# Output gates summed along rows and spread through a DRAM row, in a two-layer hybrid decoder trunk

## The chip, the core and the metric

The kernel runs on one NeuronCore of one Trainium2 chip: one TensorE, one VectorE, one ScalarE, one GpSimd, the SyncE (SP) whose queue issues most transfers, and 16 DMA engines. The metric is the device time of one execution in microseconds; the median of several runs is compared.

## The reference

Two layers of a decoder trunk on one sequence of 256 positions with a model width of 1024, all in float32. Each layer has three sub-layers: a feed-forward network (SwiGLU, 2816 hidden), a token mixing sub-layer (chunked spatial gating, sparse attention, a short convolution), and a second feed-forward network. Every sub-layer is wrapped in the same way; shift, scale and gate come from the conditioning vector c:

```python
c_act = jax.nn.silu(c)
for l in range(DEPTH):
    mod = (c_act @ mod_w[l] + mod_b[l]).reshape(Bsz, 9, D_MODEL)
    h = pre_norm_modulate(x, norm_g[l, 0], mod[:, 0], mod[:, 1])
    x = post_norm_residual(x, swiglu(h, ffn_w13[l, 0], ffn_w2[l, 0]), norm_g[l, 1], mod[:, 2], MACARON_W)
    h = pre_norm_modulate(x, norm_g[l, 2], mod[:, 3], mod[:, 4])
    y = token_mixing(h, ...)
    x = post_norm_residual(x, y, norm_g[l, 3], mod[:, 5], 1.0)
    ...

def post_norm_residual(x, y, g, gate, res_w):
    return x + res_w * gate[:, None, :] * rmsnorm(y, g)
```

The change concerns the six gates mod[:, 2], mod[:, 5] and mod[:, 8] of the two layers: each is a vector of 1024 values, the product of silu(c) with a 1024 x 1024 block of mod_w, plus a bias. It is multiplied by res_w (0.5, or 1 in token mixing) and by the norm weight norm_g before it scales y.

## The kernel before

**Weights.** The weights lie in DRAM in the order of their use, in 284 blocks of 128 partitions x 2048 float32 (1 MB). `load` (L148) issues one block on SP's queue into one of three `raw` buffers. For a matmul, `units` (L155) splits each half of the block into a rounded part `hi` (ScalarE, L162) and a remainder `lo` (VectorE, L163), eight buffers of each. `mm3` (L167) multiplies with three matmuls, hi x hi, hi x lo and lo x hi (L168 to L170), which adds up to nearly full precision.

**Sub-layers.** In `ffn` (L343) the 11 column chunks of the first weight are multiplied, passed through SwiGLU (`gate_t`, L349), transposed (`chunk_end`, L357) and multiplied by the second weight (`down`, result `yf`). In `mixing` (L485) the query and first key-value projections (`uA`, `uq`) come first, then the second key-value projection (`uB`, result `kvb`, blocks cB0 and cB1), then the compression weights `cw1` (matmuls `ph`, L754), then the attention heads. The other branches are a long generator, `bulk` (L509), whose matmuls fill in between the attention's by `fill` (L632); its first result is `cg`. At a sub-layer's end, `finish` (L313) calls `post` (L255) for each half of the positions: the norm's power of -0.5 is taken on GpSimd (`rstd`, L246), `u` is y times the gate tile (L261, L263), and x is updated (L265). `norm` (L267) scales the new x into `xn` (L274), which TensorE transposes (`xT`, L283) for the next sub-layer.

**Conditioning.** The products with silu(c) are no matmuls. At the start silu(c) is made in two forms: `cact`, 8 columns of 128 (L132 to L136), and `crow`, one row spread over all partitions by a matmul (L137 to L145). `mod_cols` (L178) makes shift and scale of a sub-layer as columns: the weight block is transposed on the host, so that one VectorE instruction multiplies it with `crow` and sums along the row (`accum_out`, L187). `mod_gate` (L198) makes a gate. A tile `acc` is cleared by GpSimd (L200) and its first partition loaded with the bias (L201). Four blocks h0 to h3 bring eight weight tiles, each multiplied by a column of `cact` and added to `acc` (L206). Then `acc` is split into `ah` (ScalarE, L212) and `al` (VectorE, L213), and matmuls with a matrix of ones (L218, L219) sum the 128 partitions and spread the sum over them. The result is multiplied into the tile `o`, named gate, which holds the norm weights, loaded on SP's queue (L210, a 4 KB row read by 128 partitions).

**Order.** Both functions are generators: every `yield` ends a step, and `mod_step` (L226) runs the next steps of a queue of jobs at places written out by hand. A gate has five steps: one for each of h0 to h2, one for h3 with the work up to `al`, one for the matmuls. In `ffn` the steps come between chunks. In `mixing` the places are counted by `MIX_STEP`: `MIX_STEP[0]` after the first two projections (L644), `[1]` and `[2]` inside the `kvb` projection after its 4th and 10th product (L724, L729), `[3]` after it (L732), `[4]` to `[11]` inside `bulk`. The order of the program gives priorities; a planner then sorts each engine's instructions by them and by the times at which it expects the operands, and places the waits. Each engine and each queue executes its list in that order.

Of the kernel before, what the change touches and what calls it, by code (L numbers as in the profile page):

```python
# [17 lines left out]
L = 2  # L18
S = 256
D = 1024  # L20
FF = 2816
P = 128
# [20 lines left out]
AFTER = (0, 0, 2, 3, 4, 5, 6, 6)  # L43
N0 = 4
S2 = 9
MIX_STEP = (2, 1, 1, 1, 0, 0, 0, 0, 1, 2, 2, 2)

N_PAIRS = L * (2 * 33 + 40 + 36)

# [22 lines left out]


@with_exitstack
def trunk(ctx: ExitStack, tc: tile.TileContext, order, x_in, c_in, wst, smalls, gmws, ng_rows, modb, lnrows, rope_c, mask_c, out):
    nc = tc.nc
    E = ctx.enter_context
    cp = E(tc.tile_pool(name="cp", bufs=1))
    rawp = E(tc.tile_pool(name="rawp", bufs=RAW_BUFS))
    wp = E(tc.tile_pool(name="wp", bufs=UNIT_BUFS))  # L80
    sp = E(tc.tile_pool(name="sp", bufs=1))
    ps_y = E(tc.tile_pool(name="ps_y", bufs=4, space=PSUM))
    ps_m = E(tc.tile_pool(name="ps_m", bufs=2, space=PSUM))
    ps_t = E(tc.tile_pool(name="ps_t", bufs=2, space=PSUM))
    V, A, G, T = nc.vector, nc.scalar, nc.gpsimd, nc.tensor

    def s4(name, shape=(P, NT, 512), dt=F32):
        return sp.tile(list(shape), dt, name=name, tag="s4", bufs=S4)
# [16 lines left out]
    def t_tile(name):  # L105
        return ps_t.tile([P, 512], F32, name=name, tag="t")


    sizes = [("cT", 8), ("ngT", L * 3 * 8), ("mbT", L * 6 * 8), ("conv", L * 12), ("pe", L * 32), ("bs", L * 4), ("cw2", L * 256)]
    tot = sum(n for _, n in sizes)  # L110
    sml = cp.tile([P, tot], F32, name="sml")
    early = 8 + L * 3 * 8 + L * 6 * 8
    crow1 = s4("crow1", (1, D))
    nc.sync.dma_start(crow1, c_in)
    nc.sync.dma_start(sml[:, :early], smalls[:, :early])
    view, at = {}, 0
# [8 lines left out]
    ones_r = cp.tile([P, P], F32R, name="ones_r")  # L125
# [3 lines left out]

    kcB = cp.tile([P, 2, 30], F32, name="kcB")  # L130
    G.memset(kcB, 0.0)
    cact = cp.tile([P, 8], F32, name="cact")  # L132
    cth = cp.tile([P, 8], F32, name="cth")
    A.activation(cth, view["cT"], AF.Tanh, scale=0.5)
    V.scalar_tensor_tensor(out=cact, in0=cth, scalar=1.0, in1=view["cT"], op0=ALU.add, op1=ALU.mult)
    V.tensor_scalar(cact, cact, 0.5, None, op0=ALU.mult)  # L136
    crow2 = s4("crow2", (1, D))  # L137
    A.activation(crow2, crow1, AF.Tanh, scale=0.5)
    V.scalar_tensor_tensor(out=crow2, in0=crow2, scalar=1.0, in1=crow1, op0=ALU.add, op1=ALU.mult)
# [1 line left out]
    crow = cp.tile([P, D], F32, name="crow")  # L141
    for h in range(2):
        pt = t_tile("crow")
# [4 lines left out]
    def load(desc, cols=2048):  # L148
        i = len(order)
        order.append(desc)  # L150
        raw = rawp.tile([P, 2048], F32, name="raw", tag="raw")
        nc.sync.dma_start(raw[:, :cols], wst[i, :, :cols])
        return raw
# [18 lines left out]
    def rows(ap2, n):  # L172
        return bass.AP(tensor=ap2.tensor, offset=ap2.offset, ap=[[0, P], [1, n]])
# [22 lines left out]
        yield  # L196

    def mod_gate(l, i):  # L198
        acc = s4("acc", (P, D))
        G.memset(acc, 0.0)  # L200
        G.dma_start(acc[0:1, :], modb[l, 3 * i + 2])  # L201
        for h in range(4):
            raw = load(("mod", l, 3 * i + 2, h))
            for u in range(2):
                k = 2 * h + u
                V.scalar_tensor_tensor(out=acc, in0=raw[:, u * D : (u + 1) * D], scalar=cact[:, k : k + 1], in1=acc, op0=ALU.mult, op1=ALU.add)  # L206
            if h < 3:
                yield
        o = cp.tile([P, D], F32, name="gate", tag="gate", bufs=1)
        nc.sync.dma_start(o, rows(ng_rows[l, i], D))  # L210
        ah, al = s4("ah", (P, D), F32R), s4("al", (P, D), F32R)
        A.activation(ah, acc, AF.Copy)  # L212
        V.tensor_tensor(al, acc, ah.bitcast(F32), ALU.subtract)  # L213
        yield
        for h in range(2):
            pt = t_tile("modg")
            hs = slice(h * 512, (h + 1) * 512)
            T.matmul(pt, lhsT=ones_r, rhs=ah[:, hs], start=True, stop=False)  # L218
            T.matmul(pt, lhsT=ones_r, rhs=al[:, hs], start=False, stop=True)  # L219
            V.scalar_tensor_tensor(out=o[:, hs], in0=pt, scalar=1.0 if i == 1 else 0.5, in1=o[:, hs], op0=ALU.mult, op1=ALU.mult)  # L220
        mods[(l, i, "g")] = o
        yield

# [2 lines left out]
    def mod_step(n=1):  # L226
        for _ in range(n):
            while jobs:
                try:
                    next(jobs[0])  # L230
                    break
                except StopIteration:
                    jobs.popleft()
# [251 lines left out]
    def mixing(l, hT, pend, nxt):  # L485
        def in_units(lo_c, n):
            return units(("in", l, ((lo_c, n),), 0)) + units(("in", l, ((lo_c, n),), 1))
# [21 lines left out]
        def bulk():  # L509
            def run(us, name, evac, hooks, **kw):  # L510
                for k, _ in enumerate(chunk_steps(evac, us, name, **kw)):
                    if k in hooks:
                        hooks[k]()
                    yield
# [3 lines left out]
            yield from run(in_units(C0 + 1024, 512), "xt", lambda t, p: V.tensor_tensor(h2[:, t], h2[:, t], p, ALU.mult), {})  # L518
            mod_step(MIX_STEP[4])
            h2T, cv = s4("h2T", (P, 4, S)), s4("cv", (P, 4, S))  # L520
# [20 lines left out]

            mod_step(MIX_STEP[5])
            ws = s2("ws", (P, 4, P))
# [198 lines left out]
        for kind in range(2):  # L742
# [4 lines left out]
            pe = view["pe"][:, (l * 2 + kind) * 16 : (l * 2 + kind + 1) * 16]  # L747
            pe = pe.unsqueeze(2).unsqueeze(3).to_broadcast([P, 16, 2, 15])
# [16 lines left out]
            A.activation(x, pg[:, :30], AF.Copy)  # L765
            h30.append(x)
        fill(F1)
        w2 = [view["cw2"][:, (l * 2 + kind) * P : (l * 2 + kind + 1) * P] for kind in range(2)]
        po = t_tile("po")
        T.matmul(po[:, :30], lhsT=w2[0], rhs=h30[0], start=True, stop=True)  # L770
        for i in range(2):
# [2 lines left out]
        h120 = s2("h120", (P, 2, 4, 15))  # L774
        A.activation(h120, h30[1].rearrange("p (g n) -> p g n", g=2).unsqueeze(2).to_broadcast([P, 2, 4, 15]), AF.Copy)
        po = t_tile("po")
        T.matmul(po[0:120, :64], lhsT=h120.rearrange("p g h n -> p (g h n)"), rhs=w2[1][:, :64], start=True, stop=True)
        A.activation(vc[:, 0], po[0:120, :64], AF.Copy, scale=0.5)
        V.scalar_tensor_tensor(out=vc[:, 1], in0=po[0:120, :64], scalar=0.5, in1=vc[:, 0].bitcast(F32), op0=ALU.mult, op1=ALU.subtract)
        fill(F1)  # L780
# [103 lines left out]
        for i in range(len(heads) + 4):  # L884
            if i < len(heads):
                t, h = heads[i]
# [78 lines left out]
def pack(inp, order):  # L965
    import numpy as np

    st = np.zeros((N_PAIRS, P, 2048), np.float32)

    def put(i, blocks):  # L970
        at = 0
        for b in blocks:
            st[i, :, at : at + b.shape[1]] = b
            at += b.shape[1]

    def kt(w, k):
        return w[k * P : (k + 1) * P]

    for i, d in enumerate(order):
        kind, l = d[0], d[1]  # L980
        if kind == "w13":
            w, j = inp["ffn_w13"][l, d[2]], d[3]
            cols = [(256 * j, 256), (FF + 256 * j, 256)]
            put(i, [kt(w, k)[:, c : c + n] for k in range(4 * d[4], 4 * d[4] + 4) for c, n in cols])
        elif kind == "w2":
            put(i, [kt(inp["ffn_w2"][l, d[2]], 2 * d[3] + k) for k in range(2)])
        elif kind == "in":
            w = inp["w_in"][l]
            put(i, [kt(w, k)[:, c : c + n] for k in range(4 * d[3], 4 * d[3] + 4) for c, n in d[2]])
        elif kind == "gate":  # L990
            w, c = inp["w_gate"][l], D * d[2] + 512 * d[3]
            put(i, [kt(w, k)[:, c : c + 512] for k in range(4 * d[4], 4 * d[4] + 4)])
        elif kind == "br":
            put(i, [kt(inp["w_branch"][l, d[2]], k)[:, 512 * d[3] : 512 * d[3] + 512] for k in range(4)])
        elif kind == "out":
            put(i, [kt(inp["w_out"][l], 2 * d[2] + k) for k in range(2)])
        elif kind == "cw1":
            put(i, [kt(inp["cmp_w1"][l, d[2]], k) for k in range(16)])
        elif kind == "mod":
            put(i, [kt(inp["mod_w"][l], 2 * d[3] + k)[:, D * d[2] : D * d[2] + D] for k in range(2)])  # L1000
        else:
            w = inp["mod_w"][l]
            put(i, [w[:, D * (3 * d[2] + j) + P * d[3] : D * (3 * d[2] + j) + P * d[3] + P].T for j in range(2)])
    return st
# [39 lines left out]
```

## Time and profile before

| | us |
|---|---|
| median of 3 runs (1299.84 to 1302.82) | 1302.6 |
| the profiled execution's own time | 1301.73 |
| span of that execution in the profile | 1300.0 |
| TensorE busy in the span | 1266.7 |
| VectorE busy | 1026.8 |
| ScalarE busy | 681.4 |
| GpSimd busy | 31.2 |
| mean granted TensorE clock, share of full speed | 0.996 |

The profile is of one execution. Starts are counted from the beginning of the span. Matmuls are pipelined: the duration of one is longer than the distance to the next. An instruction's row names the tile that it writes, an arrow, and the tiles that it reads.

### The profile page before, as it was taken

The numbers are of one execution on the slowest core, as the hardware profiler recorded it, in microseconds if no ns is written. First come the engines' busy times: TensorE is split into PE (matmuls) and PEld (weight loads), VectorE is DVE, ScalarE is ACT, GpSimd is POOL, SyncE is SP. The second block draws the span as 40 slices with busy tenths as digits, with TensorE's granted clock in tenths as the row PEclk, the third lists the DMA queues.
The fourth block names the chain that finished last, engine by engine and source line by source line (L and its number), as shares of the span: only waits on it lengthen the run. The fifth ranks groups of instructions, "written<-read, shape, count | busy, mean of one in ns | idle before, by whom it ended". The sixth has DMA issues, their size and how long they took to land.

```text
span 1300.0 us, 15997 instructions
## 1 busy us (share of the span) xinstructions
PE 1266.7 (97%) x5940; PEld 1041.0 (80%) x5940; DVE 1026.8 (79%) x1628; ACT 681.4 (52%) x1135; POOL 31.2 (2%) x53
## 2 busy tenths in 40 slices
PE   6999999999999999999999999999999999999997
PEld 4788888888778878888878888887877887888886
DVE  7977997789999698867589768586989896885553
ACT  5453446566475464544465445456674564554442
POOL 1000001000000010000010000010000000100000
PEclk9999999999999999999999999999999999999999
DMA  8966884765467448767559767366545673684540
GB/s 334 365 237 236 338 321 171 259 235 202 146 246 260 190 178 338 282 249 267 190 205 331 289 240 279 141 245 247 219 163 194 246 276 126 254 311 168 188 165 33
DMA packets 43905, 304.31 MB, mean 234 GB/s; under 512 B 5169, under 2 KB 5425, under 8 KB 8498
## 3 DMA queue, kind: packets, MB, share of 16 engines
q1 hardware_dynamic: 43634, 303.26, 62.6%
q8 instruction: 47, 0.77, 0.2%
q14 instruction: 32, 0.26, 0.1%
q0 software_dynamic: 192, 0.02, 0.0%
HBM read 302.21 MB, written 1.05 MB: 233 GB/s over the span
## 4 chain that ended last, share of the span: by engine, by line
PE 81%; DVE 9%; issue 4%; ACT 3%; DMA 2%; POOL 1%; SPq 0%; POOLq 0%; DVEq 0%; ACTq 0%
PE gu L170 11%; PE gu L168 11%; PE gu L169 11%; PE yf L170 5%; PE yf L168 5%; PE yf L169 5%; DVE lo L163 3%; PE gt L169 3%; PE gt L168 3%; PE gt L170 3%; DMA raw<-w_dram 2%; PE hT L361 1%; PE ph L754 1%; PE br L168 1%; DVE raw L187 1%
## 5 line engine op out<-in xcount | busy, mean ns | idle before, releaser
L163 DVE TENSOR_TENSOR lo<-raw,hi 128x1024 fp32r<-128x1024 f32 (+1 forms) x416 | 496.8, 1210 | 120.1 <-ACT hi L162 115.8
L162 ACT ACTIVATE hi<-raw 128x1024 fp32r<-128x1024 f32 (+1 forms) x416 | 424.7, 1048 | 235.2 <-DMA raw<-w_dram 111.6
L168 PE MATMUL gu<-hi,hT 128*128 128x512 f32 x704 | 278.9, 397 | 3.9 <-ACT hT L410 3.9
L169 PE MATMUL gu<-lo,hT 128*128 128x512 f32 x704 | 275.2, 391 | 1.7 <-DVE lo L163 1.7
L170 PE MATMUL gu<-hi,hT 128*128 128x512 f32 x704 | 275.6, 392 | 0.0
L168 PEld LDWEIGHTS gu<-hi,hT 128*128 128x128 f32 x704 | 132.7, 189 | 31.7 <-ACT hT L410 4.6
L170 PEld LDWEIGHTS gu<-hi,hT 128*128 128x128 f32 x704 | 132.5, 188 | 29.6 <-DVE hT L411 0.7
L169 PEld LDWEIGHTS gu<-lo,hT 128*128 128x128 f32 x704 | 133.0, 189 | 29.0 <-DVE lo L163 2.5
L168 PE MATMUL yf<-hi,hid 128*128 128x512 f32 x352 | 137.6, 391 | 0.0
L169 PE MATMUL yf<-lo,hid 128*128 128x512 f32 x352 | 137.2, 390 | 0.0
L170 PE MATMUL yf<-hi,hid 128*128 128x512 f32 x352 | 137.0, 389 | 0.0
L187 DVE SCALAR_TENSOR_TENSOR raw<-raw,crow 128x1024 f32<-128x1024 f32 x96 | 114.9, 1217 | 3.5 <-DMA raw<-w_dram 2.9
L353 ACT ACTIVATE ht<-gu 128x256 f32<-128x256 f32 x88 | 33.4, 383 | 158.8 <-PE gu L170 158.8
L354 DVE SCALAR_TENSOR_TENSOR ht<-ht,gu 128x256 f32<-128x256 f32 x88 | 36.4, 416 | 59.8 <-ACT ht L353 59.8
L170 PEld LDWEIGHTS yf<-hi,hid 128*128 128x128 f32 x352 | 66.1, 188 | 13.7
L169 PEld LDWEIGHTS yf<-lo,hid 128*128 128x128 f32 x352 | 66.1, 188 | 13.6
L168 PEld LDWEIGHTS yf<-hi,hid 128*128 128x128 f32 x352 | 66.1, 188 | 13.4
L168 PE MATMUL gt<-hi,hT 128*128 128x512 f32 x192 | 76.1, 396 | 0.4 <-DVE v L498 0.4
L169 PE MATMUL gt<-lo,hT 128*128 128x512 f32 x192 | 75.1, 391 | 0.3 <-DVE lo L163 0.2
L170 PE MATMUL gt<-hi,hT 128*128 128x512 f32 x192 | 75.1, 391 | 0.0
L206 DVE SCALAR_TENSOR_TENSOR acc<-raw,cact,acc 128x1024 f32<-128x1024 f32 x48 | 61.4, 1279 | 1.0 <-DMA raw<-w_dram 0.6
L821 ACT ACTIVATE pr<-sc,mx 128x128 f32<-128x128 f32 (+1 forms) x64 | 26.2, 415 | 38.4 <-DVE mx L818 38.2
(295 smaller groups left out, 1810.1 us busy)
## 6 DMA issues: line engine op xcount, KB each, us to landing
raw<-w_dram SPq DMA_DIRECT2D x276, 1024.0 KB, 4.8
raw<-w_dram SPq DMA_DIRECT2D x4, 816.0 KB, 4.3
gate<-ng_dram SPq DMA_DIRECT2D x6, 512.0 KB, 5.4
raw<-w_dram SPq DMA_DIRECT2D x4, 768.0 KB, 4.5
x<-x_dram SPq DMA_DIRECT2D x2, 512.0 KB, 4.2
ln<-ln_dram SPq DMA_DIRECT2D x2, 512.0 KB, 5.6
ws<-gmws_dram SPq DMA_DIRECT2D x2, 256.0 KB, 5.0
out_dram<-x SPq DMA_DIRECT2D x1, 512.0 KB, 2.8
```

The costliest lines, as they stand in the source:

```text
L162: A.activation(hi[:, :width], src, AF.Copy)
L163: V.tensor_tensor(lo[:, :width], src, hi[:, :width].bitcast(F32), ALU.subtract)
L168: T.matmul(o, lhsT=xh, rhs=wh, start=start, stop=False)
L169: T.matmul(o, lhsT=xh, rhs=wl, start=False, stop=False)
L170: T.matmul(o, lhsT=xl, rhs=wh, start=False, stop=stop)
L187: V.scalar_tensor_tensor(out=raw[:, j * D : (j + 1) * D], in0=raw[:, j * D : (j + 1) * D], scalar=1.0, in1=crow, op0=ALU.mult, op1=ALU.mul ...
L206: V.scalar_tensor_tensor(out=acc, in0=raw[:, u * D : (u + 1) * D], scalar=cact[:, k : k + 1], in1=acc, op0=ALU.mult, op1=ALU.add)
L353: A.activation(h, pm[:, :256], AF.Tanh, scale=0.5)
L354: V.scalar_tensor_tensor(out=h, in0=h, scalar=1.0, in1=pm[:, :256], op0=ALU.add, op1=ALU.mult)
L361: T.transpose(out=pt[:, k * S + t * P : k * S + (t + 1) * P], in_=st[j]["h"][:, t, k * P : (k + 1) * P], identity=ident)
L754: T.matmul(ph[:30, :P], lhsT=blk[:, k].rearrange("p g n -> p (g n)"), rhs=w1[:, k * P : (k + 1) * P], start=k == 0, stop=k == 15)
L821: A.activation(pr[:, br], sc[:, br], AF.Exp, scale=0.125, bias=mx[:, br : br + 1], accum_out=nsum[:, br : br + 1])
```

## The change

A gate is now made like a shift or a scale. The host transposes the weight block in such a way that partition p of the block holds the weights of the outputs 8p to 8p+7. One VectorE instruction for each of the eight tiles multiplies with `crow` and sums along the row into one column of `col`, a tile of 16 columns of which 8 are used (two copies make 128 bytes). The bias and the norm weights come as columns `mbG` and `ngG` with the small inputs, so two instructions on 8 columns finish the gate. GpSimd's queue then writes the 128 x 8 values into a 4 KB row in DRAM, in the order of the outputs, and in the next step reads this row into all 128 partitions of `o`. `acc`, `ah`, `al`, the matmuls, `cact` and the loads of bias and norm weights are gone. The compression weights `cw2` are stored in 192 columns instead of 256 per layer, and the early small inputs grow from 152 to 240 columns. `MIX_STEP` changes from 2, 1, 1, 1 to 0, 3, 1, 1 at its first four places; the total stays.

```diff
-MIX_STEP = (2, 1, 1, 1, 0, 0, 0, 0, 1, 2, 2, 2)
+MIX_STEP = (0, 3, 1, 1, 0, 0, 0, 0, 1, 2, 2, 2)
...
+    dp = E(tc.tile_pool(name="dp", bufs=1, space=bass.MemoryType.DRAM))
...
-    sizes = [("cT", 8), ("ngT", L * 3 * 8), ("mbT", L * 6 * 8), ("conv", L * 12), ("pe", L * 32), ("bs", L * 4), ("cw2", L * 256)]
+    sizes = [("ngT", L * 3 * 8), ("mbT", L * 6 * 8), ("ngG", L * 3 * 8), ("mbG", L * 3 * 8), ("conv", L * 12), ("pe", L * 32), ("bs", L * 4), ("cw2", L * 192)]
...
-    early = 8 + L * 3 * 8 + L * 6 * 8
+    early = 5 * L * 3 * 8
...
-    cact = cp.tile([P, 8], F32, name="cact")
-    cth = cp.tile([P, 8], F32, name="cth")
-    A.activation(cth, view["cT"], AF.Tanh, scale=0.5)
-    V.scalar_tensor_tensor(out=cact, in0=cth, scalar=1.0, in1=view["cT"], op0=ALU.add, op1=ALU.mult)
-    V.tensor_scalar(cact, cact, 0.5, None, op0=ALU.mult)
...
     def mod_gate(l, i):
-        acc = s4("acc", (P, D))
-        G.memset(acc, 0.0)
-        G.dma_start(acc[0:1, :], modb[l, 3 * i + 2])
+
+
+        col = cp.tile([P, 16], F32, name="gcol", tag="gcol", bufs=2)[:, :8]
         for h in range(4):
-            raw = load(("mod", l, 3 * i + 2, h))
+            raw = load(("modG", l, i, h))
             for u in range(2):
-                k = 2 * h + u
-                V.scalar_tensor_tensor(out=acc, in0=raw[:, u * D : (u + 1) * D], scalar=cact[:, k : k + 1], in1=acc, op0=ALU.mult, op1=ALU.add)
+                V.scalar_tensor_tensor(out=raw[:, u * D : (u + 1) * D], in0=raw[:, u * D : (u + 1) * D], scalar=1.0, in1=crow, op0=ALU.mult, op1=ALU.mult, accum_out=col[:, 2 * h + u : 2 * h + u + 1])
             if h < 3:
                 yield
+        at = (l * 3 + i) * 8
+        V.tensor_tensor(col, col, view["mbG"][:, at : at + 8], ALU.add)
+        V.scalar_tensor_tensor(out=col, in0=col, scalar=1.0 if i == 1 else 0.5, in1=view["ngG"][:, at : at + 8], op0=ALU.mult, op1=ALU.mult)
+        row = dp.tile([P, 8], F32, name="grow", tag="grow", bufs=2)
+        G.dma_start(row, col)
+        yield
         o = cp.tile([P, D], F32, name="gate", tag="gate", bufs=1)
-        nc.sync.dma_start(o, rows(ng_rows[l, i], D))
-        ah, al = s4("ah", (P, D), F32R), s4("al", (P, D), F32R)
-        A.activation(ah, acc, AF.Copy)
-        V.tensor_tensor(al, acc, ah.bitcast(F32), ALU.subtract)
-        yield
-        for h in range(2):
-            pt = t_tile("modg")
-            hs = slice(h * 512, (h + 1) * 512)
-            T.matmul(pt, lhsT=ones_r, rhs=ah[:, hs], start=True, stop=False)
-            T.matmul(pt, lhsT=ones_r, rhs=al[:, hs], start=False, stop=True)
-            V.scalar_tensor_tensor(out=o[:, hs], in0=pt, scalar=1.0 if i == 1 else 0.5, in1=o[:, hs], op0=ALU.mult, op1=ALU.mult)
+        G.dma_start(o, rows(row, D))
         mods[(l, i, "g")] = o
         yield
...
-        elif kind == "mod":
-            put(i, [kt(inp["mod_w"][l], 2 * d[3] + k)[:, D * d[2] : D * d[2] + D] for k in range(2)])
+        elif kind == "modG":
+            w = inp["mod_w"][l][:, D * (3 * d[2] + 2) : D * (3 * d[2] + 3)]
+            put(i, [w[:, k::8].T for k in (2 * d[3], 2 * d[3] + 1)])
```

## Rows read from the trace of the kernel before

**Rows 1.** The page: busy time, share and instructions of each engine.

```profile
PE 1266.7 (97%) x5940; PEld 1041.0 (80%) x5940; DVE 1026.8 (79%) x1628; ACT 681.4 (52%) x1135; POOL 31.2 (2%) x53
```

**Rows 2.** Busy time by stretch: PE, PEld, DVE, ACT, POOL, PEclk, DMA share, GB/s.

```profile
0.00:60.00 60.00, 47.29 (x182) 35.55 (x183) 51.78 (x94) 29.30 (x44) 3.64 (x13) 1.00 0.91 351
60.00:200.00 140.00, 140.00 (x640) 115.82 (x639) 111.48 (x153) 62.83 (x86) 0.49 (x1) 1.00 0.76 282
...
232.00:270.00 38.00, 37.77 (x227) 31.08 (x226) 27.43 (x42) 22.92 (x42) 0.00 (x0) 1.00 0.74 279
270.00:460.00 190.00, 185.76 (x895) 153.36 (x894) 166.67 (x322) 113.86 (x229) 2.30 (x4) 0.99 0.56 207
```

**Rows 3.** Timeline of TensorE at a feed-forward gate: start, duration, instruction.

```profile
151.91 0.40 PE L218 MATMUL modg<-ah,ones_r 128*128 128x512 f32 x1
152.15 0.40 PE L219 MATMUL modg<-al,ones_r 128*128 128x512 f32 x1
...
152.84 0.39 PE L168 MATMUL gu<-hi,hT 128*128 128x512 f32 x1
```

**Rows 4.** Timeline of TensorE at the gate of the first attention sub-layer.

```profile
242.85 0.40 PE L218 MATMUL modg<-ah,ones_r 128*128 128x512 f32 x1
243.18 0.62 PE L754 MATMUL ph<-raw,blk 128*30 128x128 f32 x4
244.02 0.50 PE L219 MATMUL modg<-al,ones_r 128*128 128x512 f32 x1 [0.23 <-DVE al L213]
244.45 0.62 PE L754 MATMUL ph<-raw,blk 128*30 128x128 f32 x4
245.00 0.50 PE L218 MATMUL modg<-ah,ones_r 128*128 128x512 f32 x1
...
245.66 0.62 PE L754 MATMUL ph<-raw,blk 128*30 128x128 f32 x4
```

**Rows 5.** Timeline of the start, VectorE's work on crow and its first product.

```profile
3.29 1.21 DVE L139 SCALAR_TENSOR_TENSOR crow<-crow,crow 1x1024 f32<-1x1024 f32 x1 [3.29 <-ACT crow L138]
...
6.25 0.67 DVE L140 TENSOR_SCALAR crow<-crow 1x1024 f32<-1x1024 f32 x1
...
11.49 1.22 DVE L187 SCALAR_TENSOR_TENSOR raw<-raw,crow 128x1024 f32<-128x1024 f32 x1 [0.53 <-ACT crow L145]
```

**Rows 6.** acc's memset, xn (min/median/max), transposes behind xn: timeline, by line.

```profile
853.73 0.96 POOL L200 MEMSET acc<- 128x1024 f32 x1
...
L274 DVE TENSOR_SCALAR xn<-x,rxr x24: 468/483/1153, 7.8 to 1114.7; 128x512 f32<-128x512 f32 x24
...
854.24 0.39 PE L170 MATMUL q<-hi,hT 128*128 128x512 f32 x1
855.02 1.09 PE L283 MATMUL xT<-ident,xn 128*128 128x128 f32 x8 [0.39 <-DVE xn L274]
...
  DVE xn L274: 2.4, 7
```

**Rows 7.** Groups of VectorE instructions by line and form: busy us, mean ns.

```profile
L187 DVE SCALAR_TENSOR_TENSOR raw<-raw,crow 128x1024 f32<-128x1024 f32 x96 | 114.9, 1217 | 3.5 <-DMA raw<-w_dram 2.9 <-ACT crow L145 0.5
L206 DVE SCALAR_TENSOR_TENSOR acc<-raw,cact,acc 128x1024 f32<-128x1024 f32 x48 | 61.4, 1279 | 1.0 <-DMA raw<-w_dram 0.6
L187 DVE DVE_READ_ACCUMULATOR raw<-raw,crow 128x1 f32 x96 | 7.8, 81 | 0.0
L213 DVE TENSOR_TENSOR al<-acc,ah 128x1024 fp32r<-128x1024 f32 x6 | 7.3, 1214 | 0.0
```

**Rows 8.** The gate tile: duration min/median/max in ns, first to last start.

```profile
L220 DVE SCALAR_TENSOR_TENSOR gate<-modg,gate x12: 669/682/692, 152.6 to 1170.9; 128x512 f32<-128x512 f32 x12
L261 DVE TENSOR_TENSOR u<-yf,gate x8: 681/692/692, 196.5 to 1291.5; 128x512 f32<-128x512 f32 x8
```

**Rows 9.** DMA issues of gate and acc: count, KB each, median us to landing.

```profile
gate<-ng_dram SPq DMA_DIRECT2D x6, 512.0 KB, 5.4
...
acc<-modb_dram POOLq DMA_DIRECT2D x6, 4.0 KB, 3.5
```

More of the change, by code (lines that the diff above doesn't have):

```diff
@@ L74, in trunk @@
 @with_exitstack
-def trunk(ctx: ExitStack, tc: tile.TileContext, order, x_in, c_in, wst, smalls, gmws, ng_rows, modb, lnrows, rope_c, mask_c, out):
+def trunk(ctx: ExitStack, tc: tile.TileContext, order, x_in, c_in, wst, smalls, gmws, lnrows, rope_c, mask_c, out):
     nc = tc.nc
@@ L767, in mixing @@
         fill(F1)
-        w2 = [view["cw2"][:, (l * 2 + kind) * P : (l * 2 + kind + 1) * P] for kind in range(2)]
+        w2 = [view["cw2"][:, l * 192 : l * 192 + P], view["cw2"][:, l * 192 + P : l * 192 + 192]]
         po = t_tile("po")
@@ L776, in mixing @@
         po = t_tile("po")
-        T.matmul(po[0:120, :64], lhsT=h120.rearrange("p g h n -> p (g h n)"), rhs=w2[1][:, :64], start=True, stop=True)
+        T.matmul(po[0:120, :64], lhsT=h120.rearrange("p g h n -> p (g h n)"), rhs=w2[1], start=True, stop=True)
         A.activation(vc[:, 0], po[0:120, :64], AF.Copy, scale=0.5)
@@ L1015 @@
     smalls = [
-        inp["c"].reshape(8, P).T,
         ng[:, 0::2].reshape(L * 3, 8, P).transpose(2, 0, 1).reshape(P, -1),
         inp["mod_b"].reshape(L, 3, 3, 8, P)[:, :, :2].transpose(4, 0, 1, 2, 3).reshape(P, -1),
+        ng[:, 1::2].reshape(L * 3, P, 8).transpose(1, 0, 2).reshape(P, -1),
+        inp["mod_b"].reshape(L, 3, 3, P, 8)[:, :, 2].transpose(2, 0, 1, 3).reshape(P, -1),
         inp["conv_w"].reshape(L, 3, 4, P).transpose(3, 0, 2, 1).reshape(P, -1),
@@ L1021 @@
         inp["gm_bs"].transpose(2, 0, 1).reshape(P, -1),
-        np.concatenate([inp["cmp_w2"]] * 2, 3).transpose(2, 0, 1, 3).reshape(P, -1),
+        np.concatenate([inp["cmp_w2"][:, 0], inp["cmp_w2"][:, 0], inp["cmp_w2"][:, 1]], 2).transpose(1, 0, 2).reshape(P, -1),
     ]
@@ L1025 @@
     arrays["gmws_dram"] = np.ascontiguousarray(inp["gm_ws"].transpose(0, 3, 1, 2))
-    arrays["ng_dram"] = np.ascontiguousarray(ng[:, 1::2])
-    arrays["modb_dram"] = inp["mod_b"].reshape(L, 9, 1, D)
     arrays["ln_dram"] = np.concatenate([inp["gm_ln_g"], inp["gm_ln_b"]], 1)
@@ L1038 @@
     with tile.TileContext(nc) as tc:
-        trunk(tc, order, aps["x_dram"], aps["c_dram"], wst, aps["smalls_dram"], aps["gmws_dram"], aps["ng_dram"], aps["modb_dram"], aps["ln_dram"], aps["rope_dram"], aps["mask_dram"], out)
+        trunk(tc, order, aps["x_dram"], aps["c_dram"], wst, aps["smalls_dram"], aps["gmws_dram"], aps["ln_dram"], aps["rope_dram"], aps["mask_dram"], out)
     assert len(order) == N_PAIRS
```

## The prediction

> **What bounds the kernel now.** I read the page's table of busy time first. TensorE is busy 1266.7 of 1300.0 us, VectorE 1026.8, ScalarE 681.4, GpSimd 31.2 [rows 1]. A busy TensorE is not yet a TensorE at its peak, so the second view is the timeline of a plain feed-forward stretch: matmuls of 512 columns are 0.39 to 0.40 us long there, but one starts 0.23 us after another [rows 3]. The price of a matmul is therefore its 0.23 us slot, not its length.
>
> The table of stretches comes third. In 60 to 200 us TensorE is busy 140.00 of 140.00 at a granted clock of 1.00, while VectorE has 28.5 us left; in 232 to 270 us, the head of an attention sub-layer, TensorE has 37.77 of 38.00 and VectorE 27.43 [rows 2]. In these stretches, where the gates are made, an instruction taken from TensorE shortens the kernel and one taken from VectorE only makes room. The first 60 us are different: TensorE has 47.29 of 60 and the DMA engines are 0.91 busy [rows 2]. From 270 to 460 us VectorE (166.67 of 190) stands close to TensorE, but no gate is made there.
>
> **The change part by part.**
>
> *Broadcast matmuls removed.* Each of the six gates ends in four matmuls (L218, L219) that sum the 128 partial rows and spread the sum over the partitions. In a feed-forward sub-layer the four take the slots from 151.91 to 152.84, 0.93 us, with TensorE full on both sides [rows 3]. Four of the six gates are made in feed-forward sub-layers: 4 x 0.93 = 3.7 us.
>
> In the attention sub-layers the four stand between groups of compression matmuls (ph): 0.33 us from 242.85 to 243.18, then 0.29 us by which the first ph group is longer than the second (0.84 against 0.55) because TensorE waits for al, then 0.43 and 0.66 [rows 4]. That is 1.71 us, the upper bound in one layer. The lower bound is zero, if ph then waits for its own operands. I take 1.4 us, the same sum without the wait for al, since the groups behind are transposes and ph work that already follow back to back: 2 x 1.4 = 2.8 us.
>
> *VectorE and ScalarE.* The 48 accumulations (L206, 1279 ns) become 48 products with an accumulated sum, the form of L187, at 1217 ns with a read of the accumulator of 81 ns, 1298 together [rows 7]: no difference worth a term (+0.9 us at most). Six al (1214 ns) [rows 7] and twelve last products (682 ns) [rows 8] go, 15.5 us; twelve operations on eight columns come, for which the nearest row is the 81 ns of the accumulator read and the farthest a whole 682 ns product: 1 to 8 us. I take the low end, being nearest in size. VectorE has these microseconds free anyway [rows 2], so the term is nil; if it were full there, it would be a gain of 6 to 14 us, and this stays outside the sum.
>
> [...]
>
> *The memset of acc removed.* GpSimd clears acc (0.96 us) at 853.73, just when VectorE starts xn [rows 6]; this holds at six places. xn's median is 483 ns and its longest 1153 [rows 6], so one xn in such a pair loses 0.67 us. TensorE feels it: the transposes at 855.02 follow the matmul at 854.24 by 0.78 us where a slot is 0.23, 0.39 of it shown as idle behind xn. All transposes together idle 2.4 us behind xn, in seven places [rows 6]. Without the memset I take 2.0 us, between 0 (the gap stays, as rstd is late) and 2.4.
>
> *Start-up.* Three cact operations on VectorE leave. The second operation on crow stands at 6.25, though the first, from 3.29 and 1.21 long, is done at 4.50; the first modulation product waits at 11.49 for crow [rows 5]. At most 1.75 us comes forward, at least nothing (x's own chain). I take 0.5, nearer to nothing, since xn and the raw loads arrive in the same microseconds.
>
> *The trip through DRAM.* Per gate the SP load of 512 KB (5.4 us to landing) and the GpSimd load of 4 KB (3.5) leave [rows 9]; a write of 128 pieces of 32 bytes and a spread read of 512 KB come, both on GpSimd's queue, the second waiting for the first. Bytes are the same. The nearest rows give 3.5 + 5.4 = 8.9 us; with three times that it would be 27. The first gate's last product is at 152.6 and its first use in post at 196.5 [rows 8], 44 us later; in an attention sub-layer the whole of bulk lies between. So the trip costs nothing. If the cover were gone, six trips would cost 53 us. Behind the waiting GpSimd instruction stand only the select on ws and the powers of rstd, whose sub-layer end comes later than the gate is due. Issuing 128 rows costs GpSimd at least the 0.54 us or so of a small issue and perhaps some us; at 31 us busy in all [rows 1] it is nil. SP loses one issue per gate that could hold up weights until post has freed the gate tile: a gain, bounded by 0, since I find no weight load late behind it.
>
> *The steps moved.* In attention the first two steps (loads h0, h1, four products) move behind the loads of the second key-value weights. Their order on the three raw buffers becomes cB0, cB1, h0, h1, h2, h3, then the compression weights and the first bulk weights, on the same SP queue. The count of loads up to the bulk weights is the same. Products moved: four per layer, 4.9 us of VectorE, against 10.6 us that it has free in 232 to 270 us and 2.6 us that al and the last products give back [rows 2, 7, 8]. I cost it at nothing; its cover is exactly that free time and the buffers' slack, and the price if they are gone is the third rival.
>
> *Addresses.* The column tile has 16 columns of which 8 are used, two copies; smalls shrinks by 160 bytes, cact and cth by 64, gcol adds 128: all tiles behind move 96 bytes down. No row shows what that does. One nanosecond on each of 5940 matmuls [rows 1] would be 5.9 us either way; I take zero and let the range hold it.
>
> **Sum.** 3.7 + 2.8 + 2.0 + 0.5 = 9.0 us. The profiled execution took 1301.73 us, so 1292.7 on its scale. The median of the three runs, 1302.6, lies 0.9 above it: 1293.6 us. With the small ends (0 for attention, memset and start-up) it is 1298.9, with the large ones (3.4, 2.4, 1.75) 1291.4.
>
> **The rivals.** *Given back (0.20).* The planner orders every engine's instructions anew; TensorE's freed slots in attention may turn into waits for weights, and a few new waits elsewhere eat the 3.7 us. For it: TensorE already waits for al in the middle of ph [rows 4], a sign that this place is governed by operands. Against it: the feed-forward slots have nothing to wait for. Time: 1299 to 1305, centre 1302.
>
> *A larger gain (0.04).* VectorE's relief of some 14 us and the acc, ah, al tiles it no longer holds let the planner pull weights forward in attention as well: another 6 us, 1287.6. Only the fullness of VectorE from 270 us on speaks for it [rows 2].
>
> *Weights late in attention (0.11), slower.* Four gate loads now run after the key-value weights and ahead of the compression and bulk weights. If h0 and h1 cannot land earlier because cB0 and cB1 hold the buffers until TensorE frees their converted copies, two loads of 1 MB more lie in front of the compression weights: at 351 GB/s [rows 2] 3.0 us each, 6.0 per layer, 12 in both. The attention gain goes too: 12 - 3.7 - 2.0 - 0.5 = 5.8 slower, 1308.4. It decides against the change when a layer's stall exceeds 3.1 us, and measurably at 5.1. Against it: uB's loads come earlier by the same two places, and VectorE has 10.6 us free.
>
> *Products at double price (0.01), slower.* [...] L187 speaks flatly against it [rows 7]. [...]
>
> **How the numbers follow.** The forecast has 0.64, its own range 1290 to 1298.7. A measurement of this kernel tells about 0.3% from no change, 3.9 us: faster means below 1298.7, slower above 1306.5. Faster: 0.64 + 0.04 = 0.68. Same: 0.20. Slower: 0.11 + 0.01 = 0.12. The range 1287 to 1305 leaves out the slower cases and some of the largest gain, about 0.17.
>
> **What would show it.** Right: no modg rows; matmul slots running on at 0.23 us where a gate was finished; xn pairs at 0.48 us each beside no memset, and transposes without the 0.78 us step; L187-like rows of some 1.22 us for the gate; row writes and spread reads on POOL's queue that land tens of us ahead of post. Wrong: a wait of u in post for the gate; ph or the first bulk matmuls waiting for raw; products near 2.4 us; matmul slots other than 0.23 us all through.

## The result and the profile after

The changed kernel takes 1314.9 us (median of 4 runs, 1312.34 to 1316.26) against 1302.6: a ratio of 1.0097, 95% interval 1.0083 to 1.011, about 12 us slower. The forecast was 1293.6. The profiled execution took 1312.34 us with a span of 1310.6, 10.6 us more than before.

The page after: busy time by engine, then groups of instructions (busy us, mean ns of one, idle time ahead of them and what ended it).

```profile
PE 1275.5 (97%) x5916; PEld 1038.5 (79%) x5916; DVE 1009.4 (77%) x1668; ACT 678.2 (52%) x1128; POOL 29.4 (2%) x53
...
L164 PE MATMUL gu<-hi,hT 128*128 128x512 f32 x704 | 281.7, 401 | 5.0 <-ACT hT L401 4.4
L165 PE MATMUL gu<-lo,hT 128*128 128x512 f32 x704 | 278.6, 396 | 1.4 <-DVE lo L159 1.4
L166 PE MATMUL gu<-hi,hT 128*128 128x512 f32 x704 | 278.5, 396 | 0.9 <-DVE hT L284 0.8
...
L164 PE MATMUL yf<-hi,hid 128*128 128x512 f32 x352 | 138.0, 392 | 0.0
...
L201 DVE SCALAR_TENSOR_TENSOR raw<-raw,crow 128x1024 f32<-128x1024 f32 x48 | 57.3, 1218 | 1.4 <-DMA raw<-w_dram 1.1
```

Against [rows 1], TensorE has 24 matmuls fewer and is busy 8.8 us longer; every other engine is busy for less. So the ten microseconds are not new waits of TensorE in the main: its matmuls themselves got longer. The same page of before:

```profile
L168 PE MATMUL gu<-hi,hT 128*128 128x512 f32 x704 | 278.9, 397 | 3.9 <-ACT hT L410 3.9
L170 PE MATMUL gu<-hi,hT 128*128 128x512 f32 x704 | 275.6, 392 | 0.0
L169 PE MATMUL gu<-lo,hT 128*128 128x512 f32 x704 | 275.2, 391 | 1.7 <-DVE lo L163 1.7
L168 PE MATMUL yf<-hi,hid 128*128 128x512 f32 x352 | 137.6, 391 | 0.0
```

The groups of gu moved by 4 to 5 ns, that of yf by 1.

As the second view, busy time by stretch, columns as in [rows 2]:

```profile
60.00:200.00 140.00, 140.00 (x630) 114.22 (x630) 108.78 (x159) 62.11 (x83) 1.28 (x2) 1.00 0.76 284
```

TensorE is full and the granted clock is 1.00, as before, but 630 matmuls fit where 640 did [rows 2]. A slot is what became dearer. The timeline gives it. This is the mean distance between the starts of two successive matmuls of 512 columns with the same output (those under 0.32 us apart, 2002 pairs for gu), in ns:

| stationary tile, output | before | after |
|---|---|---|
| hT, gu | 229.0 | 234.4 |
| hT, gt | 229.3 | 234.1 |
| hid, yf | 227.3 | 228.2 |
| yT, br | 231.3 | 231.8 |

Matmuls with hT as the stationary tile (the operand that TensorE loads ahead of a matmul, PEld in [rows 1]: before, the load for the matmul at 152.84 [rows 3] starts at 152.62 and takes 0.19 us; the other operand is the moving tile) take some 5 ns more, the others at most 1. The medians, which do not depend on the limit of 0.32 us, are 227 ns in all four rows before; after, they are 232 for gu and gt and 227 for yf and br. The matmuls that got longer are the ones that read two tiles on either side of the tile `gcol` that the change adds.

### The profile page after: what moved, and what is told of

Read it like the earlier page. It is cut to its first block, busy times and chain, and to the rows that moved or that the text cites. A ratio compares the mean times of both kernels' runs of the same rounds, so it can differ in the third digit from the quotient of the medians.

```text
span 1310.6 us, 15973 instructions
## 1 busy us (share of the span) xinstructions
PE 1275.5 (97%) x5916; PEld 1038.5 (79%) x5916; DVE 1009.4 (77%) x1668; ACT 678.2 (52%) x1128; POOL 29.4 (2%) x53
## 4 chain that ended last, share of the span: by engine, by line
PE 85%; DVE 7%; issue 3%; ACT 2%; POOL 1%; DMA 1%; POOLq 0%; SPq 0%; DVEq 0%; ACTq 0%
PE gu L166 11%; PE gu L165 11%; PE gu L164 11%; PE yf L164 5%; PE yf L165 5%; PE yf L166 5%; PE gt L164 3%; PE gt L166 3%; PE gt L165 3%; DVE lo L159 2%; PE br L164 1%; PE hT L352 1%; PE br L166 1%; PE br L165 1%; PE ph L745 1%
## 5 line engine op out<-in xcount | busy, mean ns | idle before, releaser
L164 PE MATMUL gu<-hi,hT 128*128 128x512 f32 x704 | 281.7, 401 | 5.0 <-ACT hT L401 4.4
L165 PE MATMUL gu<-lo,hT 128*128 128x512 f32 x704 | 278.6, 396 | 1.4 <-DVE lo L159 1.4
L166 PE MATMUL gu<-hi,hT 128*128 128x512 f32 x704 | 278.5, 396 | 0.9 <-DVE hT L284 0.8
L164 PEld LDWEIGHTS gu<-hi,hT 128*128 128x128 f32 x704 | 132.9, 189 | 35.8 <-ACT hT L401 5.3
L183 DVE SCALAR_TENSOR_TENSOR raw<-raw,crow 128x1024 f32<-128x1024 f32 x96 | 115.1, 1217 | 5.2 <-DMA raw<-w_dram 4.0
L201 DVE SCALAR_TENSOR_TENSOR raw<-raw,crow 128x1024 f32<-128x1024 f32 x48 | 57.3, 1218 | 1.4 <-DMA raw<-w_dram 1.1
```

The costliest lines, as they stand in the source:

```text
L164: T.matmul(o, lhsT=xh, rhs=wh, start=start, stop=False)
L165: T.matmul(o, lhsT=xh, rhs=wl, start=False, stop=False)
L166: T.matmul(o, lhsT=xl, rhs=wh, start=False, stop=stop)
L183: V.scalar_tensor_tensor(out=raw[:, j * D : (j + 1) * D], in0=raw[:, j * D : (j + 1) * D], scalar=1.0, in1=crow, op0=ALU.mult, op1=ALU.mul ...
L201: V.scalar_tensor_tensor(out=raw[:, u * D : (u + 1) * D], in0=raw[:, u * D : (u + 1) * D], scalar=1.0, in1=crow, op0=ALU.mult, op1=ALU.mul ...
```

## The experiments

The addresses of the tiles of before and after differ like this: hT lies 224 bytes lower, the weights' tiles raw, hi and lo 96 bytes lower, since the two 64-byte copies of `gcol` stand between them. Their distance was a multiple of 256 bytes (47360 from hT0 to hi, by the tiles' sizes: 16384 for the two hT, 6400 for gate, mraw, mcol and junk, 24576 for raw) and is now 128 more. In the experiments on the kernel before, an unused strip makes such shifts, and the order of every engine's instructions is that of before. Ratios are to the kernel before, run on the same chip (medians 1301.6 to 1302.7).

**The addresses, in both kernels.** First the changed kernel with all its old addresses (`gcol` in a pool of its own behind `sp`):

```diff
+    gcp = E(tc.tile_pool(name="gcp", bufs=1))
...
-    mhalf = cp.tile([P, 16], F32, name="mhalf")
+    mhalf = cp.tile([P, 72], F32, name="mhalf")
...
-        col = cp.tile([P, 16], F32, name="gcol", tag="gcol", bufs=2)[:, :8]
+        col = gcp.tile([P, 16], F32, name="gcol", tag="gcol", bufs=2)[:, :8]
```

> The changed kernel with 224 bytes of padding ahead of crow and the column tile moved behind all other tiles, so that crow, hT, gate, raw, hi and lo lie at exactly the addresses that they had before. Theory A (addresses: the changed kernel's tiles lie 32 bytes past a multiple of 128 and this lengthens the slot of matmuls whose stationary tile is hT from 0.229 to 0.234 us): the slots go back to 0.229 us and the time is near the sum of the prediction, 1293 us, at most 1298. Theory B (the new order of instructions, transfers or the GpSimd queue lengthens the slots): the slots stay at 0.234 and the time stays near 1314.

Measured: 1298.14 us (1297.11 to 1306.3), ratio 0.9983 (0.9968 to 0.9997), just above the 1298 that theory A allowed at most. Its row of the same stretch:

```profile
60.00:200.00 140.00, 140.00 (x640) 115.84 (x639) 109.97 (x162) 63.24 (x86) 1.84 (x3) 1.00 0.77 284
```

The 640 matmuls are back, and with the addresses the whole loss against the kernel before is gone. Now the kernel before with addresses moved: both shifts, only the one ahead of all (mhalf), only the one in between (mcol):

```diff
-    mhalf = cp.tile([P, 16], F32, name="mhalf")
+    mhalf = cp.tile([P, 24], F32, name="mhalf")
...
-        o = cp.tile([P, 8, 2], F32, name="mcol", tag="mcol", bufs=2)
+        o = cp.tile([P, 16, 2], F32, name="mcol", tag="mcol", bufs=2)[:, :8]
```

> The kernel before with 32 bytes more ahead of crow and 128 more ahead of gate; every engine's order is the same, only addresses move: all big tiles lie 32 bytes past a multiple of 128, and hT lies 128 bytes nearer to the weights' end, as in the changed kernel. Theory A: slots with hT at 0.234 us, some 3500 matmuls by 5 ns, 1302.6 + 17 = 1319 us. Theory B: no change, 1302.6.

> The kernel before with 32 bytes more ahead of crow: all big tiles move by 32 bytes together, their distances stay. Theory A1 (the place of a tile against a multiple of 64 or 128 bytes counts): as e2_before_addr, 1319 us. Theory A2 (the distance between the stationary tile hT and the moving weights counts): 1302.6. Theory B: 1302.6.

> The kernel before with 128 bytes more ahead of gate: every tile stays at a multiple of 128, but raw, hi, lo and the rest lie 128 bytes further from hT. Theory A1: 1302.6 us. Theory A2: 1319 us, slots with hT at 0.234. Theory B: 1302.6.

Measured, with both shifts: 1315.4, ratio 1.0099 (1.0085 to 1.0114). All tiles 32 bytes further: 1302.17, 1.0000 (0.9992 to 1.0009). Only 128 bytes between hT and the weights: 1315.47, 1.0101 (1.0088 to 1.0114). The stretch in this last kernel, which does exactly the work of before:

```profile
60.00:200.00 140.00, 140.00 (x630) 114.27 (x630) 111.22 (x151) 62.45 (x84) 0.00 (x0) 1.00 0.75 281
```

The 32 bytes on all tiles cost nothing that shows (ratio 1.0000); the 128 bytes more of distance cost 13.9 us. Its slots are 234.3 (gu), 234.0 (gt) and 228.1 (yf). 2112 gu at 5.3 ns, 576 gt at 4.7 and 576 others with hT at 3.7 on the mean make 16 us, a little more than the loss.

**Other distances** (the same line of `mcol` with 12, 20, 24 columns for 64, 192, 256 bytes; 40 for 512):

```diff
-        o = cp.tile([P, 8, 2], F32, name="mcol", tag="mcol", bufs=2)
+        o = cp.tile([P, 12, 2], F32, name="mcol", tag="mcol", bufs=2)[:, :8]
```

> The kernel before with 64 bytes more between hT and the weights' tiles. Theory P or Q with a gradual dependence: between the time before and that of e4_before_dist128, near 1308 us, slots near 0.2315. If only multiples of 128 bytes count: 1301.6.

> The kernel before with 192 bytes (two copies of 160 instead of 64 bytes, 320 - 128) more between hT and the weights' tiles. Nothing is left out. At 64 bytes it was +4.5 us, at 128 +13.9, at 256 and 512 nothing. Theory S (a distance counted both ways round within 256 bytes): 192 is like 64, +4 to +5, 1306 to 1307. Rival (the loss grows with the distance up to 256 and falls back there): more than at 128, 1318 or above.

> The kernel before with 256 bytes more between hT and the weights' tiles, orders unchanged; the distance from hT0 to the first hi tile becomes a multiple of 512 bytes, as the distance from the hid tiles to hi already is. Theory P (the slot depends on that distance within 512 bytes, the length of a stationary row): the slots of gu fall from 0.229 to the 0.2275 us that yf shows, 3500 x 1.5 ns = 5 us, near 1296.5. Theory Q (only the distance within 256 bytes counts, the old one being the good one): 1301.6, no change.

> The kernel before with 512 bytes more between hT and the weights' tiles. Theory P and theory Q: the same place within 512 bytes, so 1301.6 us and slots of 0.229. If the distance counts over a longer period (1024 bytes or more), another time.

| bytes added to the distance | us | ratio, 95% | slot of gu, ns |
|---|---|---|---|
| 64 | 1306.63 | 1.0043 (1.003 to 1.0056) | 230.5 |
| 128 | 1315.47 | 1.0101 (1.0088 to 1.0114) | 234.3 |
| 192 | 1317.74 | 1.0114 (1.0099 to 1.013) | 234.5 |
| 256 | 1302.53 | 1.001 (1.0 to 1.002) | 229.0 |
| 512 | 1301.81 | 1.0005 (0.9996 to 1.0014) | 228.8 |

Of these distances only those that are no multiple of 256 cost time. The guess that 192 is like 64 fell: 64 bytes cost 5.0 us, 128 cost 13.9, 192 cost 15.1, and at 256 the loss is gone. The median slots say the same: 229 ns at 64, 232 at 128, 233 at 192, and 227, as before, at 256 and 512. Whether the loss still rises from 128 to 192, as the rival had it, the two intervals do not decide. A further gain at a multiple of 512 isn't there either.

**Which tiles count.** Each product is three matmuls: hT0 with hi, hT0 with lo, hT1 with hi (L168 to L170). Here hT1 alone is moved by 128 bytes:

```diff
-        return [cp.tile([P, 8, S], F32R, name=f"hT{i}", tag=f"hT{i}", bufs=1) for i in range(2)]
+        return [cp.tile([P, 8 * S], F32R, name="hT0", tag="hT0", bufs=1).rearrange("p (k s) -> p k s", k=8), cp.tile([P, 8 * S + 64], F32R, name="hT1", tag="hT1", bufs=1)[:, 32 : 8 * S + 32].rearrange("p (k s) -> p k s", k=8)]
```

> The kernel before, with only the second of the two stationary tiles (hT1, the remainder of the normed input) 128 bytes further; hT0, the weights' hi and lo tiles and all that lies behind are where they were, counted within 256 bytes (the tile takes 256 bytes more). Nothing is left out. Theory D, each matmul by its own two operands or by the stationary tile that is loaded beside it: one of the three matmuls of each product gets longer, a third of the loss of 13.9 us that the whole distance cost: 1306 to 1307, +0.35%. Within D: if the longer slot is that of the third matmul (lo of the input with hi of the weights), the pair that a matmul itself reads decides; if it is that of the second (hi of the input with lo of the weights), during which hT1 is loaded for the next, then the loading beside the streaming does. Rival (the engines that write hi and lo collide with each other, whatever TensorE reads): no change, 1302.

Measured: 1311.07, ratio 1.0065 (1.0053 to 1.0078), 8.4 us, three fifths of 13.9 where one third was expected. The page of this kernel:

```profile
L168 PE MATMUL gu<-hi,hT 128*128 128x512 f32 x704 | 279.2, 397 | 3.9 <-ACT hT L410 3.9
L169 PE MATMUL gu<-lo,hT 128*128 128x512 f32 x704 | 279.6, 397 | 1.3 <-DVE lo L163 1.3
L170 PE MATMUL gu<-hi,hT 128*128 128x512 f32 x704 | 280.1, 398 | 0.0
```

Two of the three got longer, not one (before 397, 391, 392). By slots L169 rose from 227.4 to 232.6 and L170 from 227.2 to 233.7, while L168 went from 232.2 to 230.4. By medians L169 rose from 227 to 232, L170 from 227 to 234, and L168 stayed at 227, so the fall of its mean is one of the few long distances among them. L170 has the moved tile as its own stationary operand; L169 doesn't, but hT1 is loaded while L169 runs: in the trace of before the load for L170 starts at 153.08, as L169's matmul does, and takes 0.19 us. So neither of the two narrow forms of the theory is enough alone: a matmul's own operands and what is loaded beside it both seem to count. The edit also changes the distance between hT0 and hT1 by 128 bytes, which no other run does; what that adds to L170, beside which hT0 is loaded again, is not separated. The rival of the engines that write hi and lo is excluded, since those tiles kept their places within 256 bytes.

**The repair in the changed kernel** is one number, 256 bytes of `gcol` instead of 128:

```diff
-        col = cp.tile([P, 16], F32, name="gcol", tag="gcol", bufs=2)[:, :8]
+        col = cp.tile([P, 32], F32, name="gcol", tag="gcol", bufs=2)[:, :8]
```

> The changed kernel with one edit: the column tile has 32 columns instead of 16, so its two copies take 256 bytes and the weights lie 256 bytes, not 128, further from hT than before. Theory D (the distance between hT and the weights within 256 bytes sets the slot): 1298 us as e1_after_old_addr, slots of gu at 0.229 us. If it is the place of some other tile: stays at 1314.

Measured: 1299.65 (1296.88 to 1305.41), ratio 0.9985 (0.9974 to 0.9996).

**What is left, 2.5 to 3.5 us of the 9.** Two runs take single terms of the sum by themselves, in the kernel before. The 24 matmuls removed (the sum over partitions is left out; the last product reads al):

```diff
-            pt = t_tile("modg")
...
-            T.matmul(pt, lhsT=ones_r, rhs=ah[:, hs], start=True, stop=False)
-            T.matmul(pt, lhsT=ones_r, rhs=al[:, hs], start=False, stop=True)
-            V.scalar_tensor_tensor(out=o[:, hs], in0=pt, scalar=1.0 if i == 1 else 0.5, in1=o[:, hs], op0=ALU.mult, op1=ALU.mult)
+            V.scalar_tensor_tensor(out=o[:, hs], in0=al[:, hs].bitcast(F32), scalar=1.0 if i == 1 else 0.5, in1=o[:, hs], op0=ALU.mult, op1=ALU.mult)
```

> The kernel before without the 24 broadcast matmuls (left out of the computation: the sum over the partitions; the last VectorE product reads al instead). The prediction's first term alone: 24 slots of 0.23 us and the waits among them, 5.6 to 6.5 us less, 1295 to 1296. If freed slots are given back: 1299 to 1302.

Measured: 1293.81, ratio 0.9947 (0.9932 to 0.9961), 8.3 us. And no memset and no bias (left out): the first product writes acc.

```diff
-        G.memset(acc, 0.0)
-        G.dma_start(acc[0:1, :], modb[l, 3 * i + 2])
+                if k == 0:
+                    V.tensor_scalar(acc, raw[:, :D], cact[:, 0:1], None, op0=ALU.mult)
+                else:
...
```

> The kernel before with the first accumulation writing acc instead of adding to it, so that acc needs no memset and no bias load (the bias is left out of the gates). The prediction's memset term: 2 us less, 1299.6. Theory H (the memset and the bias load held the gate's products back behind the sub-layer's start; without them they come ahead of modulate's h): 2 to 5 us more, 1303.6 to 1306.6.

Measured: 1304.2, ratio 1.0017 (1.0009 to 1.0026): slower by 2.1 us, where the prediction had a gain of 2.0. Of these 2.1 us the profiled execution shows 0.8 in its span (1300.8 against 1300.0), and the median spans of all runs differ by 1.2 (1301.6 against 1300.4); the rest lies outside the span and stays open. In the trace the loss stands at transitions: at the starts of the two second feed-forward sub-layers and of layer 1's first one. At the first of these the changed kernel with old addresses has this timeline of VectorE (start, duration):

```profile
474.90 0.88 DVE L266 TENSOR_SCALAR xn<-x,rxr 128x512 f32<-128x512 f32 x2 [0.45 <-POOL rxr L238]
475.69 0.41 DVE L346 SCALAR_TENSOR_TENSOR ht<-ht,gu 128x256 f32<-128x256 f32 x1
476.03 1.22 DVE L202 SCALAR_TENSOR_TENSOR raw<-raw,crow 128x1024 f32<-128x1024 f32 x1
477.17 0.08 DVE L202 DVE_READ_ACCUMULATOR raw<-raw,crow 128x1 f32 x1
477.17 1.36 DVE L279 TENSOR_SCALAR h<-xT,mcol 128x128 f32<-128x128 f32 x4
```

and the kernel before has this one:

```profile
476.65 1.54 DVE L274 TENSOR_SCALAR xn<-x,rxr 128x512 f32<-128x512 f32 x2 [0.44 <-POOL rxr L246]
478.11 0.41 DVE L354 SCALAR_TENSOR_TENSOR ht<-ht,gu 128x256 f32<-128x256 f32 x1
478.55 0.42 DVE L355 TENSOR_TENSOR ht<-ht,gu 128x256 f32<-128x256 f32 x1
478.89 1.36 DVE L287 TENSOR_SCALAR h<-xT,mcol 128x128 f32<-128x128 f32 x4
```

xn does shrink from 1.54 to 0.88 us, as predicted. But a gate product of 1.22 now stands ahead of h, which starts 1.39 us after xn is done instead of 0.70. Before, the products had to wait for the memset and the bias load and so came after the transition: there the memset ends at 477.51, the bias load is issued at 477.81 and takes some 3.5 us to land [rows 9], and the first product starts at 483.04. Which of the two held them the run does not separate; the bias load is the later one. TensorE's list of waits (us in total, times, longest) names it. In the changed kernel with old addresses, and then in the kernel without memset:

```profile
PE xT L275 <- DVE xn L266: 2.3, 5, 0.6
...
PE gu L167 <- DVE hT L285: 1.5, 3, 0.6
```

```profile
PE xT L284 <- DVE xn L275: 2.4, 5, 0.6
PE gu L170 <- DVE hT L294: 2.2, 3, 0.8
```

Before, gu does not wait for that hT at all. (In the kernel without memset kva waits 0.8 for it as well.) The first row of each shows that the wait behind xn, 2.4 before [rows 6], hardly changed in total, though xn got shorter. If the product ahead of h is the cause of the new wait, taking the two steps away from the place right after `first_two` in `ffn`, and running them with the first later ones, gives the loss back:

```diff
-MSTEP = (2, 2, 1, 1, 1, 1, 1, 1, 1)
+MSTEP = (4, 2, 1, 1, 1, 1, 1, 1, 1)
...
-            mod_step(2)
```

> As e9_after_gcol256, and in the second feed-forward form the first two gate steps move from ahead of the third chunk to its end. Theory H (without the bias load the gate's products are ready early and stand on VectorE ahead of modulate's h, so that TensorE waits for hT at three feed-forward starts, 0.7 to 1 us each): 2 to 3 us less than e9, 1295 to 1296; no gate product within 5 us after xn. Theory N (the products there cost nothing): as e9, 1298.

Measured, with `gcol` at 256 bytes: 1297.11 (1293.66 to 1298.22), ratio 0.9957 (0.9944 to 0.997), 2.5 us better than the same kernel without it. h follows ht again, and gu's wait for hT is gone:

```profile
475.34 0.88 DVE L265 TENSOR_SCALAR xn<-x,rxr 128x512 f32<-128x512 f32 x2 [0.44 <-POOL rxr L237]
476.14 0.42 DVE L345 SCALAR_TENSOR_TENSOR ht<-ht,gu 128x256 f32<-128x256 f32 x1
...
476.59 0.42 DVE L346 TENSOR_TENSOR ht<-ht,gu 128x256 f32<-128x256 f32 x1
476.93 1.36 DVE L278 TENSOR_SCALAR h<-xT,mcol 128x128 f32<-128x128 f32 x4
```

This version beats both kernels. From the last yo to the first yf matmul of the next sub-layer, a stretch without a broadcast matmul, TensorE's timeline gives 35.6 and 35.5 us before (layers 0 and 1), 36.2 and 36.2 with old addresses, 36.0 and 36.0 without the memset, 35.1 and 35.1 here. From the last yf of layer 0 to the first yf of layer 1, the third such place, it is 35.2 before, 35.8 with old addresses, 35.8 without the memset and 35.1 here.

**The moved steps.** The changed kernel with old addresses, with the steps where they were:

```diff
-MIX_STEP = (0, 3, 1, 1, 0, 0, 0, 0, 1, 2, 2, 2)
+MIX_STEP = (2, 1, 1, 1, 0, 0, 0, 0, 1, 2, 2, 2)
```

> The changed kernel at the addresses of before (as e1_after_old_addr) with the first four step counts as before, 2, 1, 1, 1. Theory S (moving the steps later costs nothing, as the prediction had it): the same as e1_after_old_addr, 1298. Theory T (the first two gate loads and products ahead of the second key-value weights hold the raw buffers, and moving them back gave part of the gain): some 1 to 4 us slower, 1299 to 1302. Theory U (the move costs): faster than 1297.

Measured: 1301.03 (1298.75 to 1304.42), ratio 1.0 (0.9991 to 1.0008): without the move no gain is left to see. Its stretch at the first attention head, and TensorE's waits from 212 to 232 us (us in total, times, longest):

```profile
215.00:230.00 15.00, 12.54 (x64) 10.61 (x63) 13.29 (x24) 7.79 (x17) 2.41 (x2) 1.00 0.58 199
```

```profile
PE kva L165 <- ACT hT L284: 1.3, 1, 1.3
PE xT L275 <- DVE xn L266: 1.2, 1, 1.2
```

The same two views of the changed kernel with old addresses, that is, with the steps moved:

```profile
215.00:230.00 15.00, 14.45 (x71) 12.23 (x70) 12.75 (x25) 7.73 (x17) 1.50 (x2) 1.00 0.47 170
```

```profile
PE xT L275 <- DVE xn L266: 0.5, 1, 0.5
```

TensorE is busy 14.45 of 15, and only the second wait is left. Products at the old place crowd out xn and h at the transition once nothing holds them back; the move puts them behind it, at the price of 1.0 more of the wait of cg (below). The two ratios' intervals overlap, and the runs are of two batches. So the traces show the place, but a gain of the move (1.2 us by the spans of the two traces, 2.2 by the ratios) is not shown clear of noise.

## Why the prediction was wrong, point by point

**Addresses: the step that failed.** "... all tiles behind move 96 bytes down. No row shows what that does. ... I take zero and let the range hold it." Not all of them move alike: hT, which lies ahead of `gcol`, moves 224 bytes and the weights 96, and what counts is not how far a tile moves but its distance to the tile that it is multiplied with (all tiles moved by 32 bytes: 1302.17; 128 bytes more between hT and the weights: 1315.47). The text had a measure, 1 ns on each matmul for 5.9 us, but the matmuls with hT got 5 ns: 13.9 us alone, and in the changed kernel 14.6 to 14.8 (the ratio 1.0097 against 0.9985 and 0.9983 with the distance put right: 1.1% of 1302). The range, which reached to 1305, had no case for it, and none of the rivals was this one. The sign of error that the prediction named last, "matmul slots other than 0.23 us all through", is the one that came. With the distance put right the time, 1298.1 to 1299.7, lies inside the range, but by 2.5 to 3.5 us of gain where the sum had 9.0: the terms below missed as well.

**Broadcast matmuls: right, too small.** Alone their removal is worth 8.3 us where the sum had 6.5. Compared stage by stage in TensorE's timeline, the feed-forward parts give 4.1 (forecast 3.7) and the attention parts 4.0 (2.8; the rows' upper bound was 2 x 1.71). Why each gives a little more than the slots stays open. In the changed kernel with old addresses the attention parts give 2.5, and the feed-forward parts 1.7, or 3.6 without what three transitions lose (next point). The 1.5 that attention loses is about as long as a new wait of the kind that the rival "given back" named: cg, the first matmuls of the bulk work, now waits for weights, which it did neither before nor with the broadcast matmuls alone removed:

```profile
PE cg L165 <- ACT hi L159: 1.7, 2, 1.1
```

Why hi is later there stays open; with the steps at the old place the same wait is 0.7.

**The memset of acc: wrong sign.** The term took TensorE's 2.4 us of idle time behind xn for the memset's price. The xn pair shrank at four of the six places, but that idle time is still 2.3 us, so the lower end of the term, 0, is what came. And the memset, with the bias load, was also what held the products back; without them three transitions of the changed kernel with old addresses lose 0.6 to 0.7 us each, 1.9 in all, instead of gaining 2.0. In attention the xn pair, 1.54 us before, did not even shrink: kTl's memset moves into acc's place beside xn, in the changed kernel as two rows, of VectorE and GpSimd:

```profile
219.72 1.64 DVE L265 TENSOR_SCALAR xn<-x,rxr 128x512 f32<-128x512 f32 x2 [0.66 <-POOL rxr L237]
219.75 0.95 POOL L657 MEMSET kTl<- 64x1024 f32 x1
```

Stage by stage the changed kernel with old addresses ends 4.2 us earlier in its trace: 3.6 + 2.5 - 1.9 (the three transitions). The forecast was 9.0.

**Start-up: nothing.** The rows that answer to [rows 5], after:

```profile
3.29 1.21 DVE L135 SCALAR_TENSOR_TENSOR crow<-crow,crow 1x1024 f32<-1x1024 f32 x1 [3.29 <-ACT crow L134]
6.66 0.67 DVE L136 TENSOR_SCALAR crow<-crow 1x1024 f32<-1x1024 f32 x1
11.88 1.23 DVE L183 SCALAR_TENSOR_TENSOR raw<-raw,crow 128x1024 f32<-128x1024 f32 x1 [1.25 <-ACT crow L141]
```

The second operation on crow still comes after 6 us, 0.4 later than before, although the cact operations are gone.

**VectorE's form: right.** The 48 products take 1218 ns each, like L187's 1217 [rows 7]. No run shows a product at double price, the rival at 0.01.

**The trip through DRAM: right.** Rows of the gate tile and of the transfers, after (durations as in [rows 8], issues as in [rows 9]):

```profile
L252 DVE TENSOR_TENSOR u<-yf,gate x8: 681/692/692, 198.5 to 1302.0; 128x512 f32<-128x512 f32 x8
...
L211 POOL DMA_DIRECT2D gate<-grow x6: 533/538/557, 145.1 to 1155.4; - x6
...
gate<-grow POOLq DMA_DIRECT2D x6, 512.0 KB, 4.8
grow<-gcol POOLq DMA_DIRECT2D x6, 4.0 KB, 5.3
```

The write and the read take 5.3 + 4.8 = 10.1 us against the 8.9 worked out, and the first spread read is issued 53 us ahead of its use.

**Steps moved: costed at nil; perhaps a gain of 1 to 2 us, not shown clear of noise.** The rival in which they make weights late came true by the 1.0 us by which cg's wait grows in the trace, against its threshold of 3.1 in one layer; the waits of 1.3 of kva that the move takes away in each layer weigh more.

## What to carry to other kernels

A small tile put between two large ones changes their distance, and with it, in this kernel, the price of the matmuls that read both (slots of gu of 229.0 ns before, 234.4 after): keep the distance of a stationary and a moving tile as it was within 256 bytes, or measure it, before judging a change. If all engines but one are less busy and that one is full with fewer instructions per us, look at start-to-start distances, not at waits. A wait that is removed may have been the thing that kept low-priority work out of a critical transition; ask what will run earlier, not only what will end earlier.

## What was not expected of the hardware

In this kernel the slot of a 512-column matmul depends on the distance in SBUF between its stationary and its moving tile, counted within 256 bytes: 229.0 ns at 0, 230.5 at 64, 234.3 at 128, 234.5 at 192 (medians 227, 229, 232, 233), in executions with a mean granted clock of 0.992 to 0.997. yf, whose stationary tile hid moves with the weights, stays at 227 to 228. The tile that is loaded while a matmul runs seems to matter as well (5.2 ns on L169, whose own operands kept their distance). What in the chip makes it so, no run shows.
